# One ring of 21 score row tiles, loads of up to four rows per partition, and the copies of batch 0 issued first

## The chip, the cores and the metric

The kernel runs on one core of a Trainium2 chip (trn2). The metric is device time in microseconds. Timed runs of one kernel spread over 0.6 to 3 us here, so the changed kernel and all its variants were timed in rounds beside the kernel before, on the same chip. The TensorE clock was full (1.0).

## The reference, cut to what matters

```python
B, S, H = 8, 2048, 2560          # scores (B,S,S) f32, values (B,S,H) f32
best_j = np.argmax(scores, axis=2)
gathered = values[b_idx, best_j, :].copy()
out = np.zeros_like(values)
np.add.at(out, (b_idx, best_j, slice(None)), gathered)
```

Every row j of a batch's output is `count[j] * values[j]`, where `count[j]` is how often j was picked. So the kernel reads all scores (134.22 MB), counts, and then copies rows with count one, zeroes rows with count zero, and scales rows with a larger count.

## The kernel before

A row tile is 128 score rows of 2048 values (1 MB). VectorE finds each row's maximum and its index; TensorE counts them by one-hot matmuls. Loads go out from SyncE (queue q1), all indirect transfers from GpSimd (queue q0).

```python
def scatter_rows_in_dram(...)     # L33: HBM to HBM copy, row index per partition; an index out of bounds drops the row
...
R = 2; G = 4; NV = 6; NX = NV * H // (R * S); NB = 7      # 3 + 7 tiles of two rows per partition
...
for u in range(NT // R):                                  # count_steps, 8 loads a batch
    x = b * NT // R + u
    if x < 2 * (NX + NB) and x % (NX + NB) < NX:          # the staging space serves as score tiles at first
        x %= NX + NB
        s_tile = vbig[:, x * R * S:(x + 1) * R * S]
    else:
        s_tile = spool.tile([P, R * S], FP32, name="s_tile")[:]
    ...dma_start(out=s_tile[:, part], in_=rows_in[:, part])
    ...vector.max, vector.max_index for each of the two rows
...
first = 6 if b < 2 else 4                                 # value_steps: copies before the lists are there
for t in range(first):
    copy_once(t)
... # lists: which rows have count 0, count >= 2 (about 7 us of VectorE and TensorE)
if b == 0:
    zeros(range(nz))              # zero rows and the other 10 copies by turns
    for _ in range(10): yield     # until the staging space is free of scores
    gathers()                     # 5 gathers, then ScalarE scales, then 5 scatters
else:
    gathers(); zeros(...)
```

## Time and profile before

| | |
|---|---|
| time | 831.68 us, median of 3 (831.57 to 834.0) |
| bytes moved by DMA | 347.04 MB: 134.22 on q1, 212.67 on q0 |
| VectorE busy | 679.4 us, ends at 699 us |
| last load landed | 620.6 us (packet records) |
| last data packet | 825.95 us; the span ends 5.3 us later |

The page has one more line that matters, the group of single-row copies. Its columns are line, engine, operation, output and input, count, then busy us and mean ns of one, then the idle time before them and what ended most of it.

```profile
L33 POOL DMA_INDIRECT out_dram<-in_values_dram,ones_i x128 | 131.3, 1026 | 152.9 <-DVE m L296 114.8
```

There are 16 copies a batch, each issued over all 128 rows of a tile although only 37% of them have count one. They wait for VectorE's counts, not for each other.

### The profile page before, as it was taken

The page shows a single profiled execution, that of the slowest core. Times are in us where ns is not written, and L with a number is a line of the kernel's source. Part 1 is how long each engine was busy: PE and PEld are TensorE (multiplying, and loading weights), DVE is VectorE, ACT ScalarE, POOL GpSimd, SP SyncE. Part 2 cuts the span into 40 slices and gives each one's busy share as a digit, 9 for nine tenths or more (in the row PEclk, how much of TensorE's full clock was granted, in tenths as well). Part 3 has the DMA queues.
Part 4 walks back from the last instruction along what each step waited for, and adds up shares of the span by engine and source line. Part 5 has one row for each costly group of instructions (what it writes and reads, how often), then busy time and mean ns, then how long its engine had stood idle before and what let it go on. Part 6 is the DMA issues. An engine that isn't in the chain of part 4 may idle for free.

```text
span 831.3 us, 2048 instructions
## 1 busy us (share of the span) xinstructions
PE 14.7 (2%) x273; PEld 14.2 (2%) x273; DVE 679.4 (82%) x794; ACT 103.0 (12%) x43; POOL 272.6 (33%) x277
## 2 busy tenths in 40 slices
PE   0000000000000000000000000000000000000000
PEld 0000000000000000000000000000000000000000
DVE  7999999999999999999999999999999995000000
ACT  3000001401310001220002300013100410320320
POOL 0000642257121260061420241500516266356360
DMA  9999999999999999999999999999999999999995
GB/s 382 429 428 429 375 423 423 424 406 423 421 427 429 426 429 425 427 429 425 425 425 430 427 428 426 422 433 424 431 422 413 424 427 421 423 427 419 424 427 221
DMA packets 48111, 347.04 MB, mean 417 GB/s; under 512 B 19014, under 2 KB 19014, under 8 KB 19014
## 3 DMA queue, kind: packets, MB, share of 16 engines
q0 software_dynamic: 38736, 212.67, 61.8%
q1 hardware_dynamic: 9360, 134.22, 38.0%
q14 instruction: 13, 0.11, 0.0%
q8 instruction: 2, 0.03, 0.0%
HBM read 354.42 MB, written 300.15 MB: 787 GB/s over the span
## 4 chain that ended last, share of the span: by engine, by line
issue 35%; DVE 30%; POOL 17%; DMA 9%; another core or an unknown queue 5%; POOLq 0%; PE 0%
DVE am L189 14%; DVE mx L188 13%; POOL out_dram L33 9%; DMA out_dram<-vbig,many_i 8%; POOL out_dram L155 6%; POOL vbig L150 2%; DVE oh_lo L198 1%; DMA vbig<-in_scores_dram 1%; DVE oh L325 1%; DVE lo L194 0%; PE l_ps L343 0%; DVE oh_hi L202 0%; POOLq L479 0%; POOLq L155 0%
## 5 line engine op out<-in xcount | busy, mean ns | idle before, releaser
L189 DVE FIND_INDEX8 am<-mx,s_tile 128x8 uint32<-128x2048 f32 x116 | 265.1, 2285 | 0.0
L188 DVE MAX8 mx<-s_tile 128x8 f32<-128x2048 f32 x116 | 264.4, 2280 | 0.0
L363 ACT ACTIVATE vbig<-vbig,many_c 128x2560 f32<-128x2560 f32 x40 | 96.7, 2428 | 692.9 <-DMA vbig<-in_values_dram,many_i 692.9
L33 POOL DMA_INDIRECT out_dram<-in_values_dram,ones_i x128 | 131.3, 1026 | 152.9 <-DVE m L296 114.8
L155 POOL DMA_INDIRECT out_dram<-vbig,many_i x40 | 39.5, 988 | 238.0 <-ACT vbig L363 237.7
L150 POOL DMA_INDIRECT vbig<-in_values_dram,many_i x40 | 41.1, 1027 | 129.1 <-DMA out_dram<-vbig,many_i 81.5
L155 POOL DMA_INDIRECT out_dram<-zrow,zero_i x61 | 59.5, 976 | 18.8 <-issue 18.8
L188 DVE MAX8 mx<-vbig 128x8 f32<-128x2048 f32 x12 | 27.4, 2281 | 4.8 <-DMA vbig<-in_scores_dram 4.8
L189 DVE FIND_INDEX8 am<-mx,vbig 128x8 uint32<-128x2048 f32 x12 | 27.4, 2285 | 0.0
L198 DVE TENSOR_TENSOR oh_lo<-lo,lane_f 128x512 bf16<-128x512 uint32 x32 | 22.2, 695 | 0.4
L325 DVE TENSOR_TENSOR oh<-lo,fill_f 128x2048 f16<-128x2048 uint32 x8 | 18.3, 2292 | 0.3
L207 PE MATMUL cnt_ps<-oh_hi,oh_lo 128*128 128x16 bf16 x128 | 8.2, 174 | 579.1 <-DVE oh_hi L202 530.6
L207 PEld LDWEIGHTS <-oh_lo 128*128 128x128 bf16 x128 | 8.4, 105 | 578.9 <-DVE oh_lo L198 549.0
L189 DVE MATCH_VALUE_LOAD am<-mx,s_tile 128x8 f32 x116 | 10.7, 92 | 4.0
L202 DVE TENSOR_TENSOR oh_hi<-hi,lane_f 128x64 bf16<-128x64 uint32 x32 | 7.0, 218 | 0.0
L194 DVE TENSOR_SCALAR lo<-am 128x4 uint32<-128x4 uint32 x32 | 5.9, 185 | 1.1
L343 PE MATMUL l_ps<-put,oh 128*128 128x32 f16 x128 | 4.7, 188 | 69.0 <-DVE put L340 69.0
L343 PEld LDWEIGHTS <-oh 128*128 128x128 f16 x128 | 4.7, 104 | 70.0 <-DVE oh L325 59.6
L196 DVE TENSOR_SCALAR hi<-am 128x4 uint32<-128x4 uint32 x32 | 5.6, 175 | 0.0
L351 DVE TENSOR_SCALAR e<-l_ps 128x32 f32<-128x32 f32 x8 | 1.5, 188 | 3.1 <-PE l_ps L343 3.1
L330 DVE TENSOR_TENSOR ez<-hi,lane_f 128x256 f16<-128x256 uint32 x8 | 3.4, 419 | 0.0
L340 DVE TENSOR_TENSOR put<-ez,row_f 128x256 f16<-128x256 f16 x8 | 3.3, 418 | 0.0
(91 smaller groups left out, 61.1 us busy)
## 6 DMA issues: line engine op xcount, KB each, us to landing
s_tile<-in_scores_dram SPq DMA_DIRECT2D x58, 2048.0 KB
vbig<-in_scores_dram SPq DMA_DIRECT2D x5, 2048.0 KB
vbig<-in_scores_dram SPq DMA_DIRECT2D x2, 1024.0 KB
out_dram<-in_values_dram,ones_i POOLq DMA_INDIRECT x128
out_dram<-zrow,zero_i POOLq DMA_INDIRECT x61
vbig<-in_values_dram,many_i POOLq DMA_INDIRECT x40
out_dram<-vbig,many_i POOLq DMA_INDIRECT x40
```

The source lines that it names most:

```text
L33: return eng.add_instruction(ins)
L150: note(nc.gpsimd.indirect_dma_start(out=v, out_offset=None, in_=values_flat[:, :], in_offset=bass.IndirectOffsetOnAxis(ap=idx, axis=0), bo ...
L155: note(nc.gpsimd.indirect_dma_start(out=out_flat[:, :], out_offset=bass.IndirectOffsetOnAxis(ap=idx, axis=0), in_=v, in_offset=None, bound ...
L188: nc.vector.max(out=mx[:], in_=rows)
L189: nc.vector.max_index(out=am[:, g, :], in_max=mx[:], in_values=rows)
L194: nc.vector.tensor_single_scalar(out=lo[:], in_=am[:, :, 0], scalar=P - 1, op=ALU.bitwise_and)
L198: nc.vector.tensor_tensor(out=oh_lo[:], in0=lo[:].unsqueeze(2).to_broadcast([P, G, P]), in1=lane_f[:].unsqueeze(1).to_broadcast([P, G, P]) ...
L202: nc.vector.tensor_tensor(out=oh_hi[:], in0=hi[:].unsqueeze(2).to_broadcast([P, G, NT]), in1=lane_f[:, 0:NT].unsqueeze(1).to_broadcast([P, ...
L207: nc.tensor.matmul(out=cnt_ps[:], lhsT=oh_lo[:, g, :], rhs=oh_hi[:, g, :], start=(t == 0), stop=(t == NT - 1))
L325: nc.vector.tensor_tensor(out=oh[:], in0=lo[:].unsqueeze(2).to_broadcast([P, NT, P]), in1=fill_f[:].unsqueeze(1).to_broadcast([P, NT, P]), ...
L343: nc.tensor.matmul(out=l_ps[:], lhsT=oh[:, t, :], rhs=put[:, t, :], start=(t == 0), stop=(t == NT - 1))
L363: nc.scalar.activation(out=v, in_=v, func=mybir.ActivationFunctionType.Copy, bias=0.0, scale=mc[:, k:k + 1])
```

## The change

The intent is to keep the DMA engines fed early on: one ring of single row tiles (21 places at first: 14, and 7 in the staging space) with loads as large as the ring allows; single-row loads where tiles come free one at a time (36 to 41); and for batch 0 all 16 copies at once, while VectorE goes on with score rows and makes the lists in between.

```diff
-    R = 2
+    R = 4
-    NX = NV * H // (R * S)
-    NB = 7
+    NX = NV * H // S
+    NB = 14
+    room = ctx.enter_context(nc.sbuf_tensor([P, NV * H + NB * S], FP32))
+    turn = NX + NB
+    def place(x):
+        return NV * H + (x % turn - NX if x < 2 * turn else (x - 2 * turn) % NB) * S
+    loads, x = {}, 0
+    while x < B * NT:
+        n = 1
+        most_n = 1 if x < 2 or 2 * turn - 6 <= x < 2 * turn else 2 if x < 4 else R
+        while n < most_n and (x + n) % NT and place(x + n) == place(x) + n * S:
+            n += 1
+        loads[x] = n
+        x += n
 ... (count_steps: one row tile at a time, a load where x is in loads)
-        first = 6 if b < 2 else 4
+        first = (NT, 6, 4)[min(b, 2)]
 ...
-        yield
+        if b > 0:
+            yield
 ...
-            for _ in range(10):
+            while tiles[0] < turn + NX:
                 yield
 ...
-            if b < 2:
-                for _ in range(4):
-                    next(pending)
+            for _ in range((1, 4, 0)[min(b, 2)]):
+                next(pending)
```

More of the change, by code (lines that the diff above doesn't have):

```diff
@@ L67 @@
     consts = ctx.enter_context(tc.tile_pool(name="consts", bufs=1))
-    spool = ctx.enter_context(tc.tile_pool(name="spool", bufs=NB))
     small = ctx.enter_context(tc.tile_pool(name="small", bufs=3))
@@ L120 @@
     nc.scalar.copy(zrow[:], zero1[:].to_broadcast([P, H]))
-    vbig = consts.tile([P, NV * H], FP32)
-    nc.scalar.copy(vbig[:, NX * R * S:NV * H], zero1[:].to_broadcast([P, NV * H - NX * R * S]))
+    room = ctx.enter_context(nc.sbuf_tensor([P, NV * H + NB * S], FP32))
+    nc.scalar.copy(room[:, 0:NV * H - NX * S], zero1[:].to_broadcast([P, NV * H - NX * S]))
+    turn = NX + NB
[9 more added lines that the diff above has]
+        x += n
     ones_i = ctx.enter_context(nc.sbuf_tensor([P, B * NT], INT32))
@@ L159 @@
     vslot = [0]
+    tiles = [0]
     def stage():
-        v = vbig[:, vslot[0] * H:(vslot[0] + 1) * H]
+        v = room[:, vslot[0] * H:(vslot[0] + 1) * H]
         vslot[0] = (vslot[0] + 1) % NV
@@ L168, in count_steps @@
         am = None
-        for u in range(NT // R):
-            x = b * NT // R + u
-            if x < 2 * (NX + NB) and x % (NX + NB) < NX:
-                x %= NX + NB
-                s_tile = vbig[:, x * R * S:(x + 1) * R * S]
-            else:
-                s_tile = spool.tile([P, R * S], FP32, name="s_tile")[:]
-            rows_in = scores[b, u * R * P:(u + 1) * R * P, :].rearrange("(p r) s -> p (r s)", r=R)
-            parts = R if b == u == 0 else 1
-            for r in range(parts):
-                part = slice(r * R * S // parts, (r + 1) * R * S // parts)
-                nc.sync.dma_start(out=s_tile[:, part], in_=rows_in[:, part])
-            if u * R % G == 0:
-                am = small.tile([P, G, 8], U32, name="am")
-            for r in range(R):
-                g = (u * R + r) % G
-                rows = s_tile[:, r * S:(r + 1) * S]
-                mx = small.tile([P, 8], FP32)
-                nc.vector.max(out=mx[:], in_=rows)
-                nc.vector.max_index(out=am[:, g, :], in_max=mx[:], in_values=rows)
-                if g < G - 1:
-                    yield
-            if (u + 1) * R % G == 0:
+        for t in range(NT):
+            x = b * NT + t
+            if x in loads:
+                n = loads[x]
+                nc.sync.dma_start(out=room[:, place(x):place(x) + n * S],
+                                  in_=scores[b, t * P:(t + n) * P, :].rearrange("(p r) s -> p (r s)", r=n))
+            g = t % G
+            if g == 0:
+                am = small.tile([P, G, 8], U32, name="am")
+            rows = room[:, place(x):place(x) + S]
+            mx = small.tile([P, 8], FP32)
+            nc.vector.max(out=mx[:], in_=rows)
+            nc.vector.max_index(out=am[:, g, :], in_max=mx[:], in_values=rows)
+            if g == G - 1:
                 lo = small.tile([P, G], U32)
@@ L204, in count_steps @@
                     in1=lane_f[:, 0:NT].unsqueeze(1).to_broadcast([P, G, NT]), op=ALU.is_equal)
-                for g in range(G):
-                    t = (u + 1) * R - G + g
-                    nc.tensor.matmul(out=cnt_ps[:], lhsT=oh_lo[:, g, :], rhs=oh_hi[:, g, :],
-                                     start=(t == 0), stop=(t == NT - 1))
-                yield
+                for k in range(G):
+                    nc.tensor.matmul(out=cnt_ps[:], lhsT=oh_lo[:, k, :], rhs=oh_hi[:, k, :],
+                                     start=(t == G - 1 and k == 0), stop=(t == NT - 1 and k == G - 1))
+            tiles[0] = x + 1
+            yield
     def level_engines(rank):
@@ L344, in value_steps @@
         yield
-        yield
+        if b > 0:
+            yield
         mi = many_i[:, b * NM:(b + 1) * NM]
```

## The prediction

> **What bounds the kernel now.** I read first the page's slices and queues, to see whether an engine or the transfers set the end.
>
> ```profile
> span 831.3 us, 2048 instructions
> DMA  9999999999999999999999999999999999999995
> GB/s 382 429 428 429 375 423 423 424 406 423 421 427 429 426 429 425 427 429 425 425 425 430 427 428 426 422 433 424 431 422 413 424 427 421 423 427 419 424 427 221
> q0 software_dynamic: 38736, 212.67, 61.8%
> q1 hardware_dynamic: 9360, 134.22, 38.0%
> ```
>
> The 16 DMA engines are busy in every slice and move 420 to 430 GB/s in nearly all. 347.04 MB at 427 GB/s are 813 us of 831. So the bytes set the time, and the change moves the same bytes. Only the exceptions can be won: the first slice (start), slices 5 and 9 (375 and 406), and the last (drain). Next the windows around slices 5 and 9, 4 us each (the last two numbers are DMA share and GB/s):
>
> ```profile
> 88.00:92.00 4.00, 0.33 (x13) 0.43 (x14) 3.58 (x6) 0.00 (x0) 3.39 (x3) 1.00 0.97 398
> 92.00:96.00 4.00, 0.26 (x10) 0.15 (x6) 3.27 (x7) 0.00 (x0) 3.09 (x4) 1.00 0.94 307
> 96.00:100.00 4.00, 0.00 (x0) 0.00 (x0) 3.99 (x2) 0.00 (x0) 3.09 (x4) 1.00 0.98 346
> 100.00:104.00 4.00, 0.00 (x0) 0.00 (x0) 3.97 (x3) 0.00 (x0) 3.08 (x4) 1.00 1.02 394
> 178.00:182.00 4.00, 0.59 (x16) 0.48 (x15) 2.94 (x8) 0.00 (x0) 3.09 (x4) 1.00 1.00 397
> 182.00:186.00 4.00, 0.00 (x0) 0.00 (x0) 4.00 (x3) 0.00 (x0) 3.08 (x4) 1.00 0.99 371
> 186.00:190.00 4.00, 0.00 (x0) 0.00 (x0) 3.97 (x4) 0.00 (x0) 3.09 (x4) 1.00 1.01 392
> ```
>
> Against 427 the first four lack (29 + 120 + 81 + 33) x 4 / 427 = 2.5 us, the last three (30 + 56 + 35) x 4 / 427 = 1.1 us. A share near 1 with a low rate means packets in flight, but too few. The DMA view of 92 to 96 us shows q0 alone, 362 packets and 1.23 MB: no score load was open. The reason is how fast GpSimd issues; its timeline at the second dip:
>
> ```profile
> 172.51 0.98 POOL L33 DMA_INDIRECT out_dram<-in_values_dram,ones_i  x1 [6.49 <-DVE m L296]
> 173.80 0.98 POOL L33 DMA_INDIRECT out_dram<-in_values_dram,ones_i  x1 [0.30 <-issue]
> 175.08 2.52 POOL L33 DMA_INDIRECT out_dram<-in_values_dram,ones_i  x1 [0.30 <-issue]
> ```
>
> A copy goes out every 1.29 us. About 37% of its 128 rows have count one (a share 1/e, for 2048 random picks), so it moves 47 x 10,240 B = 0.48 MB: 374 GB/s, as the 371 of 182 to 186 shows. A stretch of copies alone is too thin by 13%.
>
> VectorE is the second clock, by freeing score rows.
>
> ```profile
> L189 DVE FIND_INDEX8 am<-mx,s_tile 128x8 uint32<-128x2048 f32 x116 | 265.1, 2285 | 0.0
> L188 DVE MAX8 mx<-s_tile 128x8 f32<-128x2048 f32 x116 | 264.4, 2280 | 0.0
> 92.66 0.19 DVE L351 TENSOR_SCALAR e<-l_ps 128x32 f32<-128x32 f32 x1 [1.03 <-PE l_ps L343]
> 167.67 2.29 DVE L189 FIND_INDEX8 am<-mx,s_tile 128x8 uint32<-128x2048 f32 x1
> ```
>
> It is never idle for a score tile; a row tile takes 4.6 us. Row tile 31, the last of batch 1, is done at 169.96 us. All its work ends at 699 us; after that only transfers run, so VectorE has slack.
>
> **What the Trainium skill says.** All four places are in "DMA: Bandwidth & Descriptors". (1) Bandwidth: the fabric gives 16 x 32 B x 850 MHz = 435.2 GB/s. The trace agrees: at most 433 in a slice, 428 over 2.65 to 90 us. No rearranging passes that. (2) Bandwidth, "Why small descriptors are slow": each packet has a fixed overhead. The packet records agree: 16,384 B take 611 ns (median of 8064), 8192 B 309 ns (256), so 302 ns per 8192 B and 7 ns fixed; 10,240 B take 385 ns (20,762), on that line; the 4 B packets, mostly dropped rows and completions, 9 ns. (3) Queues, rings and completion order: each engine takes turns between queue rows packet by packet, so larger score packets raise the share of loads against the 10 KB rows. In the trace a 2 MB load takes 4.9 us alone and about 8 us beside q0, roughly the 16:10 that equal turns would give. (4) Anatomy of one DMA: about 2 us fixed. Here the first packet of a load comes 1.0 us after issue at the start, 2 to 4 us after it beside q0.
>
> **The change, part by part.**
>
> *Larger loads.* From the order of the built program: 43 loads (25 of 4 rows, 1 of 3, 8 of 2, 9 of 1) for 65 (63 of 2, 2 of 1). Data packets fall from 65 x 128 = 8320 to 43 x 128 = 5504 if a 32 KB row stays one packet. 2816 x 7 ns / 16 engines = 1.2 us, and 22 x 16 completion packets x 9 ns / 16 = 0.2 us. What is saved before row tile 42 is lost in a gap (below); rows 42 on take 25 loads in place of 43, which leaves 18 x 128 x 7 / 16 = 1.0 us and 0.2: **-1.1 us**.
>
> *First dip.* Copies of batch 0 now go out 16 in a row, from 86 to 108 us: 374 GB/s. But one load of 4 row tiles (32 to 35) is released by row tile 14 at 78.8 us, just as its forerunner ends: 32 x 1.0486 MB / 0.4288 + 2.65 us of start = 80.9. It and row 36 keep q1 busy past 92 us. Then single-row loads 37 to 41 are released by each tile that VectorE ends, at about 91, 101, 105, 110 and 116 us; VectorE comes to row 16 6 us earlier as the lists are put off. Ledger from 80.9 us: by 100 us there are 6.3 MB of loads and 3.4 of copies, 9.7, against 8.2 that the engines can move; by 112 us 16.1 against 13.3. The dip goes: +2.5 us won for the moment.
>
> *The lull after it.* From row 42 on a tile needs one of 14 places. Load 42 to 45 needs row tiles 28 to 31 done; before, rows 40 to 43 could start after 27 and 29. The lists between tiles save VectorE the 1.0 us wait on TensorE, so row 31 ends at 169.0 and data flows at about 171. All that can be moved until then is 42 row tiles (44.0 MB) and batch 0's q0 bytes (212.67 / 8 = 26.6 MB): 70.6 MB. That ends at 2.65 + 70.6 / 0.427 = 168 us. So the engines stand idle for some **3 us at 168 to 171**. At 171 us the kernel before has also moved 70.7 MB (packet records): what the first dip gave is handed back whole. Net **0**.
>
> *Second dip.* At 171 us a 4.2 MB load now lies beside the six lone copies of batch 1, in place of a 2 MB one and a pause. It lasts until the gathers (1.3 MB each) join at about 182. By 190 us 78.7 MB are moved; before, 78.4. I take **-0.9 us** of the 1.1.
>
> *The rest.* Zero rows now follow the 16 copies, and the gathers of batch 0 wait for row tiles 21 to 26 in place of 21 to 25: inside the same ledger. Batches 2 to 7 keep their order; q0 is backlogged there, with batch 1's bytes ending only near 292 us in the trace. A load of 4 is issued with 10 tiles left, 46 us of VectorE, against some 13 us to land at a 32:10 share: no stall. The tail (q0 alone from 620 us) is untouched.
>
> Sum: 831.7 - 0 - 0.9 - 1.1 = **829.7 us**.
>
> **Rivals.** *A: the lull isn't there*, because the chain gather, ScalarE, scatter reaches past 171 us with other work beside it. For it: the scatters of batch 0 ran thinly from 153 to 176 us before. Against it: the byte ledger caps what exists at 171 us whatever the order. If my release times are 2 to 3 us late, the first dip's 2.5 us stay won: 827. *B: the lull is worse.* From 120 to 171 us no load is open, so q0 must carry it alone, and each scatter waits for its gather (landing, 2.43 us on ScalarE, issue, 2 to 4 us). By my chain the scatters stay only 2 us ahead of need; should the loads win more turns early, or gathers come late, 2 to 4 us more are idle: 832 to 834. *C: 32 KB packets starve q0, or are cut into 16 KB.* In the first case the gathers come in bursts but bytes don't change, so it costs little with a backlog; in the second the 1.1 us go: 830.8. *D: VectorE stalls on larger loads.* It would have to lose tens of us of slack before the tail, 133 us of q0 work, felt it. I give it 3%.
>
> **Range and chances.** The terms are 1 to 3 us each, and runs of the kernel before spread from 831.6 to 834.0. A gives 827, B 834, the middle 829.7: range **827.0 to 832.5**. Faster by 2% needs 815 us: 347 MB at 430 GB/s alone are 807, and start and drain take some 10 more, so it would take a gapless stream at once above today's rate: 1.5%. Slower by 2% (848) needs a stall of 16 us that nothing above yields: 1.5%.
>
> **What would show it.** In the changed kernel: 88 to 108 us at 420 GB/s or more; a DMA share well below 1 somewhere within 164 to 172; no rate under 410 from 174 to 190; 32 KB packets at about 1215 ns and 6192 packets on q1 (43 x 144); VectorE ending within 2 us of 699. Wrong if q1 shows more packets, if the hole lies elsewhere or is over 5 us, if VectorE idles on loads, or if the mixed rate between 200 and 700 us differs from 426 by over 2 GB/s: that alone is 2.3 us.

## The result, and the profile after

The changed kernel took **832.15 us** (median of 4, 831.55 to 832.53); the kernel before, in all its runs by then, 831.87. The ratio is 0.9997, with a 95% interval of 0.998 to 1.0015: the same. The time is inside the predicted range, at its upper end; of the forecast 2.0 us nothing is to be seen.

The page of the changed kernel, span, rate by slice and queues:

```profile
span 830.4 us, 2035 instructions
GB/s 380 448 431 425 405 411 423 410 396 412 429 427 428 413 431 434 433 417 426 425 429 431 429 430 423 419 434 424 429 427 419 424 427 421 425 426 424 424 426 222
q0 software_dynamic: 38736, 212.67, 61.7%
q1 hardware_dynamic: 6192, 134.22, 37.8%
```

Slices and windows count a packet where it starts. With 32 KB packets, of 1.2 us each, a single figure can therefore stand well off: the 448 of slice 2 is 433 GB/s when each packet is counted by its share, as the ledger below does.

The bytes are the same and q1's packets fell from 9360 to 6192, as forecast. Slice 5 rose from 375 to 405, but slices 8, 9 and 14 fell (410, 396, 413). The windows of 4 us show where; busy times of PE, PEld, DVE, ACT and POOL come first, clock, DMA share and GB/s last:

```profile
92.00:96.00 4.00, 0.00 (x0) 0.10 (x1) 3.89 (x10) 0.00 (x0) 3.39 (x3) 1.00 1.01 420
96.00:100.00 4.00, 0.58 (x16) 0.47 (x15) 3.96 (x3) 0.00 (x0) 3.09 (x4) 1.00 1.01 413
100.00:104.00 4.00, 0.00 (x0) 0.00 (x0) 3.93 (x8) 0.00 (x0) 3.09 (x4) 1.00 1.03 384
...
152.00:156.00 4.00, 0.00 (x0) 0.00 (x0) 3.97 (x4) 3.39 (x2) 1.00 (x1) 1.00 0.87 364
...
168.00:172.00 4.00, 0.47 (x6) 0.40 (x6) 3.40 (x19) 0.00 (x0) 0.93 (x1) 1.00 0.94 347
...
180.00:184.00 4.00, 0.00 (x0) 0.00 (x0) 3.96 (x4) 0.00 (x0) 3.09 (x4) 1.00 0.93 374
184.00:188.00 4.00, 0.00 (x0) 0.00 (x0) 3.97 (x4) 0.00 (x0) 3.09 (x4) 1.00 1.04 392
188.00:192.00 4.00, 0.00 (x0) 0.00 (x0) 3.97 (x4) 0.00 (x0) 3.03 (x4) 1.00 0.98 378
```

The first dip is gone up to 100 us (307 and 346 became 420 and 413; 100 to 104 us stays thin), the hole at 168 to 172 is there, a smaller hole came at 152 to 156, and the second dip stands as it was. VectorE's groups show that it is no suspect:

```profile
L196 DVE MAX8 mx<-room 128x8 f32<-128x2048 f32 x128 | 291.6, 2278 | 4.6 <-DMA room<-in_scores_dram 4.6
L197 DVE FIND_INDEX8 am<-mx,room 128x8 uint32<-128x2048 f32 x128 | 292.5, 2285 | 0.0
```

Its only wait for a load (4.6 us) is the first, as before (4.8).

**A ledger.** To compare kernels I use one figure throughout: the time *lost* by T, that is T less the bytes moved by T divided by 428 GB/s (the rate of q1 alone in the kernel before). It is summed from the trace's packet records, a packet under way counted by its share. A thin stretch adds to it; the 10 KB packets of q0 alone, at 424 GB/s, add about 1% of their time. The last column is the end of the last data packet.

| us lost by | 80 | 120 | 172 | 200 | 300 | 620 | 815 | last packet |
|---|---|---|---|---|---|---|---|---|
| before | 2.34 | 4.94 | 5.64 | 6.89 | 7.30 | 8.17 | 10.53 | 825.95 |
| after | 1.89 | 3.15 | 5.73 | 6.68 | 7.47 | 7.86 | 9.69 | 824.21 |
| after, again | 1.86 | 3.98 | 6.16 | 7.11 | 7.87 | 8.50 | 10.79 | 825.63 |
| lull filled | 1.86 | 3.97 | 5.34 | 6.60 | 7.31 | 7.69 | 9.59 | 823.43 |
| lull deeper | 1.86 | 4.07 | 7.24 | 13.11 | 13.41 | 14.55 | 17.36 | 834.17 |
| order alone | 2.42 | 6.52 | 7.05 | 8.37 | 8.69 | 9.37 | 11.41 | 826.17 |
| ring alone | 1.93 | 3.75 | 6.58 | 7.63 | 8.28 | 8.53 | 10.51 | 824.94 |
| 1 row per load | 3.44 | 4.29 | 6.73 | 7.82 | 8.34 | 10.08 | 11.86 | 827.35 |
| at most 2 rows | 2.41 | 3.55 | 5.52 | 6.63 | 7.13 | 7.98 | 9.80 | 824.44 |
| small loads late | 1.86 | 3.27 | 5.71 | 6.89 | 7.40 | 9.11 | 11.08 | 825.81 |
| fewer lone copies | 1.95 | 3.56 | 5.31 | 5.89 | 7.01 | 7.35 | 9.15 | 823.61 |
| all filled | 2.01 | 3.55 | 3.90 | 5.03 | 6.41 | 6.71 | 8.69 | 824.59 |
| all filled, again | 2.14 | 3.95 | 4.22 | 5.14 | 6.37 | 6.92 | 9.13 | 824.23 |

### The profile page after: what moved, and what is told of

Same layout as the page of the kernel before. It is cut to its first block, busy times and chain, and to the rows that moved or that the text cites. A ratio compares the mean times of both kernels' runs of the same rounds, so it can differ in the third digit from the quotient of the medians.

```text
span 830.4 us, 2035 instructions
## 1 busy us (share of the span) xinstructions
PE 14.7 (2%) x273; PEld 14.1 (2%) x273; DVE 679.0 (82%) x794; ACT 101.3 (12%) x43; POOL 275.7 (33%) x277
## 3 DMA queue, kind: packets, MB, share of 16 engines
q1 hardware_dynamic: 6192, 134.22, 37.8%
HBM read 354.42 MB, written 300.15 MB: 788 GB/s over the span
## 4 chain that ended last, share of the span: by engine, by line
DVE 71%; DMA 13%; issue 8%; POOL 6%; another core or an unknown queue 1%; POOLq 0%; PE 0%; DVEq 0%
DVE am L197 32%; DVE mx L196 30%; DMA room<-in_values_dram,many_i 8%; DMA out_dram<-room,many_i 4%; POOL out_dram L33 3%; DVE oh_lo L204 2%; POOL out_dram L170 2%; DVE oh L331 2%; POOL room L165 1%; DVE lo L200 1%; DMA room<-in_scores_dram 1%; DVE oh_hi L208 0%; DVE hi L202 0%; DVE put L346 0%
## 5 line engine op out<-in xcount | busy, mean ns | idle before, releaser
L196 DVE MAX8 mx<-room 128x8 f32<-128x2048 f32 x128 | 291.6, 2278 | 4.6 <-DMA room<-in_scores_dram 4.6
L197 DVE FIND_INDEX8 am<-mx,room 128x8 uint32<-128x2048 f32 x128 | 292.5, 2285 | 0.0
L370 ACT ACTIVATE room<-room,many_c 128x2560 f32<-128x2560 f32 x40 | 96.8, 2427 | 693.2 <-DMA room<-in_values_dram,many_i 693.1
L170 POOL DMA_INDIRECT out_dram<-room,many_i x40 | 40.7, 1019 | 238.6 <-ACT room L370 235.8
L165 POOL DMA_INDIRECT room<-in_values_dram,many_i x40 | 42.1, 1053 | 120.5 <-DMA out_dram<-room,many_i 71.9
L197 DVE MATCH_VALUE_LOAD am<-mx,room 128x8 f32 x128 | 11.8, 92 | 4.3
L321 DVE TENSOR_SCALAR rank<-base,off_ps 128x16 f32<-128x16 f32 x16 | 3.0, 241 | 0.0
L344 DVE TENSOR_TENSOR put<-em,row_f 128x128 f16<-128x128 f16 x8 | 2.3, 292 | 0.3
```

The source lines that it names most:

```text
L165: note(nc.gpsimd.indirect_dma_start(out=v, out_offset=None, in_=values_flat[:, :], in_offset=bass.IndirectOffsetOnAxis(ap=idx, axis=0), bo ...
L170: note(nc.gpsimd.indirect_dma_start(out=out_flat[:, :], out_offset=bass.IndirectOffsetOnAxis(ap=idx, axis=0), in_=v, in_offset=None, bound ...
L196: nc.vector.max(out=mx[:], in_=rows)
L197: nc.vector.max_index(out=am[:, g, :], in_max=mx[:], in_values=rows)
L370: nc.scalar.activation(out=v, in_=v, func=mybir.ActivationFunctionType.Copy, bias=0.0, scale=mc[:, k:k + 1])
```

## The experiments

Theory one, the ledger: DMA time lost in the middle is paid at the end one for one, and the change trades one thin place for another. Theory two: the end is set by something that losses in the middle don't touch. Twelve runs were made, in five rounds each: ten new kernels, and two of them once more (the changed one and the last). All were correct.

### Nothing changed: how far can one see?

> The changed kernel once more, unedited, timed in five rounds beside the kernel before. It says how far the two can be told apart, and how much the byte ledger of one kernel (bytes moved by a given time, from the packet records) wanders from one profile to the next. Either theory: ratio 0.9975 to 1.001. If the 0.9 us by which the changed kernel is ahead of the one before at 815 us in the first profile is real, it is there again within 0.4 us; if it is chance, it is not.

Measured: 832.82 us, ratio 1.0001 (0.9988 to 1.0014). By 815 us this profile had lost 10.79 us against 9.69 of the first one, and so it is 0.3 behind the kernel before, not 0.8 ahead. The 0.8 us were chance. The ledgers of two profiles of one kernel thus lay up to 1.1 us apart (0.8 at 120 us, 0.4 at 172 us, 1.1 at 815 us); a ratio is known to about 0.0014, 1.2 us. Finer conclusions need either a size above that or several profiles that agree.

### The lull filled

```diff
-        most_n = 1 if x < 2 or 2 * turn - 6 <= x < 2 * turn else 2 if x < 4 else R
+        most_n = 1 if x < 2 or 2 * turn - 6 <= x < 2 * turn + 6 else 2 if x < 4 else R
```

> The changed kernel with row tiles 42 to 47 loaded one at a time (six loads of 1 MB for one of 4 and one of 2), so that they are released by row tiles 28 to 33 one by one, from about 153 us, and not by tile 31 at 168.5 us. Theory one, the ledger: engine time lost in the middle is paid at the end one for one. The hole at 168 to 172 us closes (DMA rate 415 GB/s or more there), the loss at 171 us falls from 6.3 to under 4.5 us, and the time falls by 1.5 to 2.5 us against the changed kernel: about 830, ratio to before 0.996 to 0.999. Theory two, the end is set by something that mid-run losses do not touch (the slowest DMA engine, which keeps a backlog through the thin stretches, or the drain): the hole closes and the time stays within 0.5 us of the changed kernel.

Measured: 831.41 us, ratio 0.9987 (0.9974 to 1.0). Its windows in the two holes:

```profile
152.00:156.00 4.00, 0.00 (x0) 0.00 (x0) 3.96 (x4) 3.45 (x2) 0.99 (x1) 1.00 0.83 343
...
168.00:172.00 4.00, 0.46 (x6) 0.39 (x6) 3.41 (x20) 0.00 (x0) 1.94 (x2) 1.00 1.00 418
```

The hole at 168 closed as expected (347 to 418 GB/s). The other stayed, since load 42 is issued only at 154.7 us. The time fell by 1.4 us against the changed kernel, a little under the 1.5 to 2.5 forecast; at 172 us the ledger shows 0.4 to 0.8 us less lost. At 171 us it stands at 5.3, where under 4.5 was forecast. Theory one is favoured, but the effect is too small to decide alone.

### The lull deeper

```diff
-... else 2 if x < 4 else R
+... else 2 if x < 4 else 6 if x == 2 * turn else R
```

> The changed kernel with row tiles 42 to 47 as one load of six, so that it is released only by tile 33, at about 187 us. A dose in the other direction. Theory one: between 168.5 us and the first data of batch 1's copies at about 175 us nothing runs, and after that copies alone until 190: 4 to 7 us more are lost, and the time rises by that, to 836 to 839. Theory two: the ledger shows the loss at 190 us, but the time rises by less than half of it.

Measured: 841.44 us, ratio 1.0102 (1.0087 to 1.0117).

```profile
168.00:172.00 4.00, 0.47 (x6) 0.40 (x6) 3.40 (x19) 0.00 (x0) 0.93 (x1) 1.00 0.58 238
172.00:176.00 4.00, 0.00 (x0) 0.10 (x1) 3.83 (x10) 0.00 (x0) 3.39 (x3) 1.00 0.68 202
176.00:180.00 4.00, 0.59 (x16) 0.48 (x15) 3.29 (x8) 0.00 (x0) 3.09 (x4) 1.00 0.74 215
180.00:184.00 4.00, 0.00 (x0) 0.00 (x0) 3.96 (x4) 0.00 (x0) 3.08 (x4) 1.00 1.02 287
```

With no load open the engines ran at half rate for 16 us. The ledger at 200 us is 6.0 us above that of the changed kernel run beside it (13.11 against 7.11), at 815 us 6.6; the last packet is 8.5 us later, and the time 8.6. **This decides for theory one** for a loss of this size: 6 us lost 650 us before the end are paid in full. It even came out about 2 us dearer than the loss itself, in the drain after 815 us, which I can't explain. For losses under 1 us no run decides it alone.

### The order alone, and the ring alone

Order alone is the kernel before with `first = (NT, 6, 4)[min(b, 2)]`, one `yield` less for batch 0 and `for _ in range((1, 4, 0)[min(b, 2)])`; ring alone is the changed kernel with these three undone.

> The kernel before (its old tiles and loads of 2 rows) with the new order of batch 0 alone: 16 single-row copies first, lists between row tiles. Theory one: the thin stretch of 92 to 104 us, which cost 2.5 us, is not cured by the order alone, since no load is released until row tiles 16 and 17 are both done at about 100 us: copies alone run there at under 400 GB/s, so 1 to 2 us of it stay; the loads of tiles 40 to 45 still fill 152 to 172 us, so no hole: 830.5 to 832. Theory two: 831.5 to 832.5. Rival within theory one: if the order is what cured the first dip, the loss at 120 us is 3.3 us as in the changed kernel and not 5.2.

> The changed kernel's ring and loads with the old order (6 copies of batch 0, then its lists at once, then copies and zero rows by turns). Ledger theory: the singles released by row tiles 15 to 20 cure part of the first dip (loss at 120 us 4 to 5, against 5.2 before and 3.3 to 4.2 after); the cap on bytes until row tile 31 stays, so the hole at 168 to 172 us is there and the loss at 174 us is again 6 to 7: 832 to 833.5. Rival: the order is what made the hole (batch 0's bytes done too early), so without it there is none, and the time is under 831.5.

Order alone: 833.35 us, ratio 1.0013 (0.9999 to 1.0027), slower than forecast. The windows of the first dip:

```profile
96.00:100.00 4.00, 0.59 (x16) 0.48 (x15) 3.97 (x6) 0.00 (x0) 3.09 (x4) 1.00 0.96 320
100.00:104.00 4.00, 0.00 (x0) 0.00 (x0) 3.93 (x8) 0.00 (x0) 2.91 (x4) 1.00 1.00 332
104.00:108.00 4.00, 0.00 (x0) 0.00 (x0) 4.00 (x2) 0.00 (x0) 2.95 (x4) 1.00 0.99 346
```

It made the dip deeper: 4.1 us lost from 80 to 120 us, against 2.6 before. Copies alone, with no zero rows between them and no load open, ran at 320 and 332 GB/s from 96 to 104 us though the DMA share is 0.96 and 1.00. The packet records say how that fits: there q0's 10,240 B packets took 467 and 475 ns on average, where 385 is the median. In the kernel before it was 481 and 450 ns from 92 to 100 us. By these records the engines were occupied and the packets slow. What makes them slow isn't shown.

Ring alone: 832.94 us, ratio 1.0013 (1.0 to 1.0027), as forecast. It lost 1.8 us from 80 to 120 us; the eleven profiles with the ring (without the misbuilt one below) lost 0.85 to 2.2 there, the kernel before 2.6. So it is the ring that eases the first dip, and not the order; that its single-row loads 36 to 41 do it is read from the windows, no run isolates them. And the ring brings the lull, with the old order too:

```profile
164.00:168.00 4.00, 0.00 (x0) 0.00 (x0) 3.97 (x4) 1.61 (x1) 1.50 (x2) 1.00 0.87 366
168.00:172.00 4.00, 0.26 (x4) 0.26 (x4) 3.48 (x12) 0.00 (x0) 0.00 (x0) 1.00 0.87 307
```

The rival, that the order made this hole, falls. The smaller one at 152 to 156 us is the order's in this ring: from 152 to 160 us ring alone lost 0.21 us, the changed kernel 0.68 and 0.77. Both parts alone are 1.1 us slower than the kernel before (intervals that just reach 1); together they even out.

### What a packet costs

One row per load everywhere (`R = 1`); at most two (`R = 2`, lull filled); and the filled kernel with single-row loads from tile 36 on (`2 * turn - 6 <= x` alone).

> The changed kernel with one row tile per load throughout (128 loads, 16,384 packets of 8 KB), so the lull is filled as in e2_lull_filled (831.4 us), and only the packet size differs from that kernel's 47 loads and 6016 packets. Theory one, packet overhead is paid everywhere: 10,368 packets x 7 ns / 16 = 4.5 us more, 835 to 837. Theory two, the 7 ns are paid only where the score queue runs alone, and hidden where two queues take turns: only the 24 more loads before row tile 36 count, 24 x 128 x 7 / 16 = 1.3 us, 832 to 833.5; the loss from 200 to 600 us is as in e2_lull_filled, 1.4 us.

> e2_lull_filled with at most two row tiles per load (72 loads, 9216 packets), as many as the kernel before used, in the new ring. Paid everywhere: 3200 packets x 7 / 16 = 1.4 us more than e2_lull_filled, 832.8. Paid only alone: 8 loads before row 36, 0.4 us: 831.5 to 832. The larger loads were then worth nothing from batch 2 on.

> e2_lull_filled with one row tile per load from row tile 36 to the end, so only loads that run beside the other queue get small packets: rows 48 to 127 in 10,240 packets of 8 KB in place of 2944. Paid per packet everywhere: 7296 x 7 / 16 = 3.2 us more than e2_lull_filled, 834 to 835.5. Half hidden, as the ledger of e4_rows1 from 200 to 620 us suggests (2.3 against 1.2 lost): 1.1 us more, 832 to 833. Hidden: no change, 831 to 832.

| | packets of scores | time | ratio | interval |
|---|---|---|---|---|
| lull filled | 6016 | 831.41 | 0.9987 | 0.9974 to 1.0 |
| at most 2 rows | 9216 | 832.14 | 0.9999 | 0.9985 to 1.0013 |
| small loads late | 13,312 | 833.57 | 1.0020 | 1.0007 to 1.0034 |
| 1 row per load | 16,384 | 835.70 | 1.0047 | 1.0033 to 1.0060 |

The times rise with the packets, by 1.0, 2.7 and 5.0 us (ratios x 832), near the 1.4, 3.2 and 4.5 of 7 ns per packet, each known to about 1.6 us. So the times alone fit 7 ns paid everywhere. The ledger can separate the stretches. Up to 80 us q1 is alone:

```profile
2.65:80.00 77.35, 0.76 (x12) 0.78 (x12) 73.88 (x68) 2.65 (x2) 0.00 (x0) 1.00 1.01 432
```

is the filled kernel, and with one row per load it is

```profile
2.65:80.00 77.35, 0.76 (x12) 0.79 (x12) 73.80 (x68) 2.65 (x2) 0.00 (x0) 1.00 1.01 421
```

that is 1.6 us for 2930 packets more (340 of them completions) on 16 engines, about 9 ns each. Beside q0, from 300 to 620 us, the loss is 1.7 us in both kernels with 8 KB packets, 0.85 and 0.87 with 16 KB (at most 2 rows; before), and 0.39, 0.63, 0.38, 0.25 and 0.34 with 32 KB (after, after again, lull filled, ring alone, fewer lone copies: mean 0.40; all filled had 0.30 and 0.55). Two profiles stand outside: order alone, 16 KB, with 0.68, and lull deeper, 32 KB, with 1.14. Some 60 row tiles load there, in about 7670, 3870 and 2375 data packets; so (1.72 - 0.86) x 16 / 3800 and (0.86 - 0.40) x 16 / 1495 are 3.6 and 4.9 ns: **about 4 ns per data packet by the ledger, not 7**, where two queues take turns, with the completions counted in. By that neither theory in the expectation of the run with one row per load holds as put: the cost is paid everywhere, at half the size. But the ledger at 815 us holds only 0.2, 1.5 and 2.3 of the 1.0, 2.7 and 5.0 us by which the times rose. The last packets came 1.0, 2.4 and 3.9 us later, so most of the rest was lost in the drain, for no reason that is shown. Whether 4 or 7 ns is the price in time is thus not settled.

### The second dip, and the copies that stand alone

```diff
-        first = (NT, 6, 4)[min(b, 2)]
+        first = (NT, 4, 4)[min(b, 2)]        # on top of the filled lull
```

> e2_lull_filled with 4 copies and not 6 before batch 1's first gather, aimed at the second dip (376 to 397 GB/s at 180 to 192 us). If that dip comes from copies standing alone in the queue, fewer of them make it smaller: the loss from 180 to 190 us falls from 1.1 to 0.5 us and the time to 830.5 to 831.2. If it comes from the mix of copies and gathers too, or from q0 not having its data ready, nothing changes: 831.2 to 831.8.

Measured: 831.24 us, ratio 0.9992 (0.9978 to 1.0006). From 172 to 200 us 0.6 us were lost, with the lull filled alone 1.3; its window of 188 to 192 us, where that kernel has 397 GB/s:

```profile
188.00:192.00 4.00, 0.00 (x0) 0.00 (x0) 3.97 (x3) 0.00 (x0) 3.08 (x4) 1.00 1.02 424
```

In time the 0.7 us can't be told from the filled lull. The two runs of "everything filled" below hold the same edit. The three profiles with four lone copies lost 0.5 to 0.8 us from 180 to 200 us, the seven others with the ring 0.85 to 1.14 (deeper lull and the misbuilt run left out). So fewer lone copies do make this dip smaller. But from 200 to 300 us the same three lost 1.1 to 1.4 us, the filled lull 0.7 and the changed kernel 0.8: the gain was given back in batch 2.

### What a dropped row costs

```diff
+        if 3 <= b <= 6:                                           # on top of the filled lull
+            for _ in range(16):
+                scatter(zrow[:], none_i[:, 0:1], free_running)     # none_i: all 1 << 24, out of bounds
```

> e2_lull_filled (ratio to before 0.9987) with 64 more scatters, 16 in each of batches 3 to 6, whose 128 indices are all out of bounds: nothing is written, 8192 more dropped rows. It prices a dropped row, which the copies contain 81 of in 128. If it costs what its packet record says, 9 ns on one of 16 engines, the 8192 rows and 1024 completion packets cost 9216 x 9 / 16 = 5.2 us and the time is 836 to 837.5. If it costs about 18 ns, as the 390 GB/s of a copies-only stretch suggests (a copy of 47 rows then takes 1.23 us and not 1.19), it is 9 to 10 us: 840 to 842. Were the stretch slow only because GpSimd issues one copy per 1.29 us, the record's 9 ns hold and 5.2 us is right.

Measured: 851.19 us, ratio 1.0234 (1.022 to 1.0248): twice the dearer forecast, and **the experiment was misbuilt**. The build's order put 20 of the 64 scatters at the very start, and the last 16 stood in a row at 686 to 709 us, when no load was left to fill the time GpSimd takes to issue them:

```profile
695.00:700.00 5.00, 0.59 (x16) 0.58 (x16) 2.51 (x16) 0.00 (x0) 3.99 (x4) 1.00 0.87 340
700.00:705.00 5.00, 0.00 (x0) 0.00 (x0) 0.00 (x0) 0.00 (x0) 3.87 (x4) 1.00 0.64 234
705.00:710.00 5.00, 0.00 (x0) 0.00 (x0) 0.00 (x0) 0.00 (x0) 3.79 (x4) 1.00 0.40 144
```

This is starvation by issue: it cost about 8 us between 700 and 750 us. (By 815 us the run had lost 15 us more than the filled lull; the rest was not taken apart.) The accident at the start gives a price all the same. Of the 2880 packets of those 20 scatters, 1220 ran beside full loads by 80 us, where this profile had lost 2.52 us and the seven others with the same loads 1.86 to 1.95: 0.6 x 16 / 1220 is about 8 ns per dropped row or completion, near the 9 ns of their records. (The other 1660 came in one burst at 80 to 84 us; by 90 us the whole excess is 1.5 to 2.2 us, 8 to 12 ns each.) With 9 ns, copies alone could reach about 405 GB/s. They show 384 even with copies waiting (100 to 104 us in the changed kernel), and again the packet records hold the difference: the 150 packets of 10,240 B there took 420 ns on average and not 385. Why they do stays open.

### Everything filled

```diff
-        most_n = ... else 2 if x < 4 else R                       # on top of the filled lull
+        most_n = ... else 2 if x < 4 or 25 <= x < 36 else R
-        first = (NT, 6, 4)[min(b, 2)]
+        first = (11, 4, 4)[min(b, 2)]                             # 5 copies of batch 0 between its gathers
-                if rest:                                          # in zeros()
+                if rest and b > 0:
```

> e2_lull_filled with the other thin places filled too: 11 copies of batch 0 first and 5 later between its gathers (for the hole at 152 to 156 us, 343 to 364 GB/s, and the copies-only stretch at 100 to 108), 4 copies of batch 1 before its first gather as in e8_fewer_lone, and loads of at most 2 rows for row tiles 25 to 35 (for the 0.5 us lost at 80 to 90 us). Ledger theory: each is worth 0.4 to 0.8 us, the loss at 200 us falls from 6.8 to about 5, and the time to 829.5 to 830.5, ratio to before 0.996 to 0.9985: better than both kernels, but by under 0.5%. If what is filled early is lost again to later thin places, the loss at 200 us falls and that at 600 us does not: 831 to 832.

> e10_all_filled once more, unedited. Its interval (0.9971 to 0.9998) only just excludes 1, and its last data packet came as late as 824.6 us although its byte ledger at 815 us was 0.9 us ahead of e2_lull_filled, whose last packet came at 823.4. If the gain is real the ratio is again 0.997 to 0.999 and the loss at 200 us again 5 to 5.5. If the late last packet was chance, it comes at 822.5 to 823.5 here; if the drain takes the ledger's gain back by rule, at 824 or later.

Measured: 830.80 and 831.64 us; the ratios are 0.9985 (0.9971 to 0.9998) and 0.9985 (0.9971 to 0.9999). Both holes are closed:

```profile
152.00:156.00 4.00, 0.00 (x0) 0.00 (x0) 3.96 (x4) 2.22 (x2) 0.98 (x1) 1.00 1.01 412
...
168.00:172.00 4.00, 0.47 (x6) 0.39 (x6) 3.40 (x19) 1.08 (x1) 1.94 (x2) 1.00 1.01 429
```

The first time lies just above the 829.5 to 830.5 of the ledger theory, the second in the range of the other outcome; both ratios are at the forecast's upper end. At 200 us this kernel has lost 5.0 and 5.1 us, 1.8 less than the changed one. Of this 1.3 are left at 300 us, and the time is 1.2 us shorter. It beats the kernel before, twice with an interval below 1, and by 0.15%, far inside what counts as the same. Against the changed kernel (0.9997 and 1.0001) the gain is as small, and no interval was taken between the two. Its last packet came at 824 us or later both times though the lull-filled kernel, with 0.5 to 0.9 us more lost at 815 us, ended at 823.4: the drain took that back. What sets the drain was not settled: over the last 5 to 9 us of data the packets in flight fall from about 15 to one, and 3 to 6 us are lost there.

## Why the prediction was right or wrong

The range and the mechanism (347 MB at a fixed rate, only thin places to win) held. The centre was 2.0 us too hopeful against the two measured ratios, 0.9997 and 1.0001, each good to about 1.3 us. Of the signs named beforehand these came: 6192 packets, 32 KB ones at 1213 ns, VectorE ending at 698 us, and the same rate from 200 to 700 us (426.2 and 425.8 GB/s, before 425.8). These did not: 420 GB/s from 88 to 108 us (it held only to 96), a share well below 1 in the lull (0.94), and no rate under 410 from 174 to 190. By its steps, with both profiles of the changed kernel against the one of before:

- **The reading of the thin stretches.** A copy is issued every 1.29 us, but "in flight, but too few" doesn't explain 307 and 346 GB/s, which lie below the 374 of that issue rate. At 92 to 100 us q0's 10,240 B packets took 481 and 450 ns and not 385, which the prediction didn't look at.
- **First dip: goes.** Half right. From 80 to 120 us 1.3 and 2.1 us were lost, 2.6 before: 0.5 to 1.3 us won and not 2.5. The forecast ledger at 100 and 112 us said nothing at all would be lost; copies alone ran at 384 GB/s although more were waiting. The runs of the parts add what the prediction left mixed: it is the ring that eases the dip, and the new order by itself deepens it.
- **The lull hands it back whole, net 0.** Right in place, kind and sum: the share fell to 0.94 and the rate to 347 GB/s at 168 to 172 us, and at 172 us the changed kernel had lost 5.73 and 6.16 us, the one before 5.64. But the sum is right because both its terms were too large: there were no 3 us of idle engines, and from 120 to 172 us 1.5 to 1.9 us more were lost than before. That these two misses cancel is luck. The small excess is rival B: scatters of batch 0 came late and left the hole of 152 to 156 us (364 GB/s), before the cap on bytes. I had put the scatters 2 us ahead of need.
- **Second dip: -0.9 us.** This step failed in size. The loss from 172 to 200 us fell from 1.25 to 0.95 in both profiles: 0.3 us. The prediction let the lone copies run beside the 4 MB load from about 175 us. They did not get far: from 176 to 180 us the packet records show 50 packets of q1 and 55 of q0, near enough turn by turn, but 34 of the 55 are dropped rows or completions. So q1 moved 381 GB/s and q0 50, and the copies stood alone once the load had ended. That larger score packets made it so is not shown: in the filled lull and in the three runs with smaller packets 91 to 104 rows of q0 went out from 176 to 180 us and not 21, and yet 1.1 to 1.3 us were lost from 172 to 200 us.
- **Larger loads: -1.1 us from row 42 on.** By the ledger this term was mis-sized. (The unrounded sum is 1.2.) The packets came as forecast (32,768 B, 1213 ns), and alone on the engines they saved 0.45 us by 80 us, what 7 to 9 ns give. Beside q0 a packet costs about 4 ns by the ledger and not 7, which leaves 0.5 us; from 300 to 620 us 0.24 and 0.48 us were gained. The times of the runs with smaller packets do not exclude 7.
- **Batches 2 to 7: q0 is backlogged there.** Wrong in one place that I had not looked at. The four lone copies of batch 2 fall between two 4 MB loads and stand alone. Windows of 280 to 288 us, before:

```profile
280.00:284.00 4.00, 0.18 (x4) 0.26 (x4) 3.90 (x10) 0.00 (x0) 0.00 (x0) 1.00 1.00 419
284.00:288.00 4.00, 0.07 (x3) 0.00 (x0) 3.97 (x6) 0.00 (x0) 2.97 (x3) 1.00 1.04 436
```

and after:

```profile
280.00:284.00 4.00, 0.25 (x4) 0.26 (x4) 3.93 (x10) 0.00 (x0) 1.04 (x1) 1.00 0.97 371
284.00:288.00 4.00, 0.00 (x0) 0.00 (x0) 3.96 (x4) 0.00 (x0) 3.08 (x4) 1.00 0.99 402
```

From 200 to 300 us the changed kernel lost 0.79 and 0.76 us, the one before 0.41, and the ring with loads of one or two rows 0.50 to 0.52. So 0.1 to 0.3 us are given back by the large loads themselves. From 276 to 292 us the five kernels with loads of one or two rows lost 0.11 to 0.22 us, and the nine profiles with loads of four 0.37 to 0.75, but for one of 0.20 (the deeper lull). The load size does it, then; that it is the lone copies between the loads is read from the traces.

- **Rivals.** A (no lull) fell, and B was right in part. C, in its first half, was taken too lightly: large packets do hold q0 back, and in batch 2 that cost a few tenths. D did not happen.

By 300 us the changed kernel had thus lost 0.2 to 0.6 us more than the one before, where -0.9 and the first part of the packets' -1.1 were forecast; the 0.2 to 0.5 us that it gained from 300 to 620 us are inside the noise.

## What to carry to other kernels

When the transfers bound a kernel as here, write down for each moment all the bytes that can be moved by then; a rearrangement that moves bytes earlier can only shift the hole to where the next release comes, and here a hole of 6 us in the middle cost its full length at the end. Where the rate is low though the engines are occupied, look at how long a packet takes before you blame the issue. Large loads saved 4 to 9 ns a packet here but are released later and hold back the other queue, so try small loads where the other queue is thin and large ones where both are full. Near the ceiling, run the same kernel twice and look at both traces before explaining a microsecond.

## What the Trainium skill lacked or had wrong

- "DMA: Bandwidth & Descriptors", section "Why small descriptors are slow", gives a fixed overhead of about 3 cycles per packet and no time for large packets. The runs show 7 to 9 ns by record (8192 B 309 ns, 16,384 B 611 ns, 32,768 B 1213 ns), about 9 ns in the byte ledger where one queue runs alone, and only about 4 ns where two queues take turns.
- The same page, "Queues, rings and completion order", tells of turns by packet, but no page says whether a dropped row of an indirect DMA takes a turn as well. The counts of the changed kernel from 176 to 180 us fit that it does: q0 had 55 packets to q1's 50 and yet 50 GB/s to 381, since 34 of the 55 were 4 B packets.
- No page prices a dropped row. The runs show a 4 B packet of 9 ns, and about 8 ns per packet in time where all-dropped scatters ran beside loads.
- No page says that a copy's packets can take longer where copies stand alone. The runs show 420 to 481 ns on average in such stretches (92 to 104 us) for a 10,240 B packet whose median is 385 ns; the cause is open.
- The profile's HBM write count includes dropped rows: with 8192 of them more it rose from 300.15 to 384.04 MB, by 8192 x 10,240 B, while the queues moved 0.04 MB more. No page says so.
- "DMA: Bandwidth & Descriptors" gives a first byte of about 1 us for DMAs from GpSimd. Here the first packet of the first indirect copy came 4.2 us after the instruction began (85.98 to 90.2 us in the kernel before, with loads in flight).
- No page tells of the drain: over the last 5 to 9 us of data the packets in flight fall from about 15 to one, which hides or takes back half a microsecond either way.
